# Expert weights laid out by the host in six 1 MB pieces, each loaded by one transfer with 8 KB in a row for each partition

## The chip, the cores and the metric

The kernel runs on one core of a Trainium2 chip. The metric is the device time of one execution in microseconds (us). Names of engines: PE multiplies matrices, DVE and ACT work element by element, POOL is the general-purpose engine (it also issues the indirect transfers), SP issues all other transfers. The data move on 16 DMA engines that the queues share.

## What is computed

One decoder layer on 2048 tokens of width 1024. A token mixer (gated linear attention and a gated delta rule, joined by an output projection) is followed by a layer norm; then comes a mixture of experts, and a second layer norm. The change touches the experts alone, whose reference, cut, is:

```python
D_MODEL, N_EXPERTS, TOP_K, D_EXPERT = 1024, 64, 2, 512

def expert_block(blk):                  # up to 128 tokens that chose expert e
    xb, e = blk
    hid = jax.nn.silu(xb @ w_gate[e]) * (xb @ w_up[e])
    return hid @ w_down[e]
...
y = jnp.einsum('nkd,nk->nd', y_assign, gate)      # two experts a token
x = _layer_norm(ALPHA_DN * x + y, ln2_g[l], ln2_b[l])
```

Everything is float32. One expert has 2 MB in each of `w_gate` (1024 x 512), `w_up` (1024 x 512) and `w_down` (512 x 1024), so that all 64 experts have 384 MB, and every one of them is read once.

## The kernel before

`mixer_front` and `mixer_out` compute the mixer, the first layer norm and the router, token tile by token tile. The last part of `mixer_out` (`project` and `route`, lines 860 to 925) loads for each tile of 128 tokens `ma`, `mb` (line 878) and `x` (line 880), multiplies by `w_out` (line 898), normalises, stores the row `x_d` (line 905) and transposes it for the router; POOL adds the bias of the norm (line 215) and scatters the tile's two routing entries a token into a table (`tab_d`, line 191).

**Experts.** `experts` runs through 52 tiles of up to 128 tokens: 3 for experts 0 to 2, then by falling size 6 tiles of three experts with two tiles each (a double), 28 of one expert (solo) and 15 tiles in which two experts with at most 64 tokens share the two halves of the partitions (a pair). A tile's stages: POOL gathers the tokens' rows (`xg<-x_d`, line 1344), PE transposes them and multiplies by gate and up (`gu`, line 1349), ACT and DVE form the hidden values, PE multiplies by down (`y`), DVE adds with the gate (line 1436), and POOL scatters the result (`y_d<-xg`, line 1439). Five buffers `xg` serve for gathering and for the result, so a gather waits for the scatter of five tiles before.

**Weights.** The class `Weights` cuts an expert into six pieces of [128, 4, 512] float32 (1 MB, 8 KB a partition). Pieces 0 to 3 hold two rows of gate and two of up for each partition, pieces 4 and 5 two rows of down. The order of loads (`load`, lines 1189 and 1193) and splits into a high and a low part (`split`, ACT at line 1203, then DVE or, for piece 5, POOL at line 1205) is written down beforehand by `slot_plan`: 20 slots of 1 MB are shared by pieces that are landing and by high and low parts, and a load waits until the last user of its slot is done. Pieces of a pair are used as they land, without a split. The first nine pieces are loaded inside `mixer_out`.

A piece of gate and up is loaded by two transfers, a piece of down by one:

```python
for j, w in enumerate((w_gate, w_up)):
    self.nc.sync.dma_start(raw[:, 2 * j:2 * j + 2, :],
                           w[e].rearrange("a (p k) c -> p (a k) c", k=8)
                           [:, 2 * i:2 * i + 2, :])
```

For gate and up, partition p owns eight rows of 2 KB in a row in DRAM (16 KB), of which a piece takes two, that is 4 KB. For down, partition p owns four rows of 4 KB, of which a piece takes two, 8 KB.

All of these transfers stand in SP's one queue, in the program's order. The program gives SP's transfers eight semaphores in turn, and a transfer is issued only after the one eight places before it has landed; so at most eight are under way. A scheduler orders each engine's instructions within the limits of the dependencies that the code lays down; the order of PE in the experts is fixed by hand.

At the end `overflow` treats blocks that did not fit the plan, in a loop whose count is read from memory, and `Final.norm` reads `y_d` (line 1575, 16 transfers of 1 MB with 8 KB in a row for each partition), adds and normalises.

Of the kernel before, what the change touches and what calls it, by code (L numbers as in the profile page):

```python
# [21 lines left out]
D = 1024  # L22
# [5 lines left out]
NE = 64  # L28
# [13 lines left out]
@with_exitstack  # L42
def hybrid_kernel(ctx, tc, x, w_in, w_gk_up, b_gk, conv_w, a_log, dt_bias, gla_norm_g, gdn_norm_g,
                  w_out, ln1_g, ln1_b, w_router_group, b_router_group, w_router_expert,
                  b_router_expert, w_gate, w_up, w_down, ln2_g, ln2_b, out, dbg=None, upto=9):
    nc = tc.nc
    dbg = dbg or {}
    dram = lambda name, shape, dt=F32: tc.dram_tile(shape, dt, name=name)
    dr = {n: dram(n + "_d", shape) for n, shape in (
        ("aT", [NT, 128, 4, 128]), ("bT", [NT, 128, 12, 128]), ("va", [NT, 128, 512]),  # L50
        ("ra", [NT, 128, 512]), ("zb", [NT, 128, 512]), ("ma", [NT, 128, 512]),
        ("mb", [NT, 128, 512]),
        ("na", [NT, 4, 128, 128]), ("at", [NT, 128, 512]), ("kd", [NT, 128, 512]),
        ("vp", [NT, 128, 512]), ("td", [2, NT, 4, 4, 32, 32]))}
    x1_d = dram("x1_d", [S, D])
    y_d = dram("y_d", [2 * S, D])
    tab_d = dram("tab_d", [S * NE, 2], I32)

    consts = ctx.enter_context(tc.tile_pool(name="consts", bufs=1))
    mixer = ctx.enter_context(ExitStack())  # L60
    mc = mixer.enter_context(tc.tile_pool(name="mixerc", bufs=1))
    jp = mc.tile([128, 128], I32, name="jp")
    nc.gpsimd.iota(jp, pattern=[[1, 128]], base=0, channel_multiplier=-1)
    ident = consts.tile([128, 128], F32, name="ident")
    nc.vector.tensor_scalar(ident, jp, 0.0, None, op0=OP.is_equal)
    gt = Gates(tc, nc, mc, jp, a_log, dt_bias)

    rt = Routing(tc, nc, consts, jp, tab_d)
    scan = Scan(nc, gt, mc, ident, dr)
    mixer_front(tc, nc, gt, scan, ident, x[0], w_in[0], conv_w[0], gla_norm_g, gdn_norm_g,  # L70
                w_gk_up[0], b_gk, dr)
    for n, t in dr.items():
        if n in dbg:
            nc.sync.dma_start(dbg[n], t)
    if upto <= 2:
        return
    late = ctx.enter_context(tc.tile_pool(name="late", bufs=1, side="right", reuse_waits="tile"))
    rt.row = late.tile([1, NE], I32, name="row")
    rt.more = late.tile([1, 257], I32, name="more")
    rt.list = late.tile([128, 1], I32, name="list0")  # L80
    land = ctx.enter_context(ExitStack())
    weights = Weights(tc, nc, land, w_gate[0], w_up[0], w_down[0])
    mixer_out(tc, nc, rt, scan, weights, ident, x[0], w_out[0], ln1_g, ln1_b, w_router_group[0],
              b_router_group, w_router_expert[0], b_router_expert, dr, x1_d)
    if "x1" in dbg:
        nc.sync.dma_start(dbg["x1"], x1_d)
    if "gates" in dbg:
        nc.sync.dma_start(dbg["gates"], rt.choice[:, :, :, 1].bitcast(F32))
    if upto <= 3:
        return  # L90
    mixer.close()
    weights.open("p5b", range(EARLY, EARLY + 9))
    blocks = land.enter_context(tc.tile_pool(name="blocks", bufs=1, reuse_waits="tile"))
    listing = Order(tc, nc, rt, ident, blocks)
    listing.rank()
    experts(tc, nc, rt, listing, weights, ident, x1_d, y_d, tab_d)
    land.close()
    fix = ctx.enter_context(tc.tile_pool(name="p7fix", bufs=1, side="right", reuse_waits="tile"))
    final = Final(nc, fix, ln2_g, ln2_b)
    overflow(tc, nc, rt.more, ident, w_gate[0], w_up[0], w_down[0], x1_d, y_d, tab_d)  # L100
    final.norm(tc, ident, y_d, out[0])


# [3 lines left out]
class Routing:  # L107
    def __init__(self, tc, nc, consts, jp, tab_d):
        f = lambda name, shape, dt=F32: consts.tile(shape, dt, name=name)
        self.tab = tab_d  # L110
        self.count = f("count", [128, 128])
        self.iota = self.count[:, :NE]
        self.choice = f("choice", [128, NT, 2, 2], I32)
        self.gates = self.choice[:, :, :, 1].bitcast(F32)
        nc.gpsimd.iota(self.choice[:, :, :, 0], pattern=[[256, NT], [1, 2]], base=0, channel_multiplier=2)
        self.known = f("known", [128, NT, 2])
        self.mine, self.base = f("mine", [128, NT, 2], BF16), f("base0", [128, NT])
        self.before = f("before", [128, 128], BF16)
        nc.vector.tensor_scalar(self.before, jp, 0.0, None, op0=OP.is_gt)
        self.ones = f("ones_b", [128, 128], BF16)  # L120
        nc.vector.memset(self.ones, 1.0)
        self.carry = [f(f"carry{i}", [128, NE]) for i in range(2)]
        nc.vector.memset(self.carry[0], 0.0)
        self.turn = 0
        self.slots = {}
        with tc.tile_pool(name="padp", bufs=1) as pool:
            ii = pool.tile([128, 128], I32, name="iota_i")
            nc.gpsimd.iota(ii, pattern=[[1, 128]], base=0, channel_multiplier=0)
            nc.vector.tensor_copy(self.count, ii)
            ki = pool.tile([128, NT, 2], I32, name="known_i")  # L130
            nc.gpsimd.iota(ki[:, :, 0], pattern=[[0, NT]], base=0, channel_multiplier=1)
            nc.gpsimd.iota(ki[:, :, 1], pattern=[[128, NT]], base=-2 * S, channel_multiplier=0)
            nc.vector.tensor_copy(self.known, ki)
            pad = pool.tile([128, 2 * S * NE // 128], I32, name="pad")
            nc.gpsimd.memset(pad, PAD)
            nc.sync.dma_start(flat(tab_d, [[2 * S * NE // 128, 128], [1, 2 * S * NE // 128]]), pad)
# [1026 lines left out]
class Weights:  # L1163


    def __init__(self, tc, nc, ctx, w_gate, w_up, w_down):
        self.tc, self.nc, self.ctx = tc, nc, ctx
        self.w = w_gate, w_up, w_down
        self.raw, self.where = {}, {}
        units = [(1, 1)] * FIRST + [(1 + (q[0] < DOUBLE), len(q)) for q in place_order()]  # L1170
        self.todo, uses = sequence(units)
        self.whole = [units[pos][1] == 2 for _, pos, _, _ in self.todo]
        self.events = slot_plan(uses, self.whole)
# [8 lines left out]

    def load(self, m, slot, e):
        raw = self.raw[m] = self.tile(slot, F32)
        w_gate, w_up, w_down = self.w
        e, i = ds(e, 1), self.todo[m][3]
        if i < 4:
            for j, w in enumerate((w_gate, w_up)):
                self.nc.sync.dma_start(raw[:, 2 * j:2 * j + 2, :],
                                       w[e].rearrange("a (p k) c -> p (a k) c", k=8)  # L1190
                                       [:, 2 * i:2 * i + 2, :])
        else:
            self.last = self.nc.sync.dma_start(
                raw.rearrange("p (k a) b -> p k (a b)", k=2),
                w_down[e].rearrange("a (p k) c -> p (a k) c", k=4)[:, 2 * (i - 4):2 * (i - 4) + 2, :]).ins

    def take(self, m):
        return self.raw.pop(m)
# [281 lines left out]
                fetch(n + 2)  # L1480


def overflow(tc, nc, row, ident, w_gate, w_up, w_down, x1_d, y_d, tab_d):

    with ExitStack() as es:
        fix = es.enter_context(tc.tile_pool(name="p6fix", bufs=1, reuse_waits="tile"))
# [3 lines left out]
        v = nc.vector  # L1490
# [3 lines left out]
        n = nc.values_load(row[0:1, 256:], min_val=0, max_val=2 * S // 128)  # L1494
        with tc.For_i(0, n) as i:
            e = nc.values_load(row[0:1, ds(2 * i, 1)], min_val=0, max_val=NE - 1)
# [4 lines left out]
            wu = [wts.tile([128, 2, D // 2], F32, name=f"ou{j}") for j in range(4)]  # L1501
            wg = [wts.tile([128, 2, D // 2], F32, name=f"og{j}") for j in range(4)]
            wd = [wts.tile([128, 2, D], F32, name=f"od{j}") for j in range(2)]
            for j in range(4):
                for t, w in ((wg[j], w_gate), (wu[j], w_up)):
                    nc.sync.dma_start(t, w[ds(e, 1)].rearrange("a (p k) c -> p (a k) c", k=8)
                                      [:, 2 * j:2 * j + 2, :])
            for j in range(2):
                nc.sync.dma_start(wd[j], w_down[ds(e, 1)].rearrange("a (p k) c -> p (a k) c", k=4)
                                  [:, 2 * j:2 * j + 2, :])  # L1510
            tok = work.tile([128, 1], I32, name="otok")
            v.tensor_scalar(tok, ids, 1, None, op0=OP.arith_shift_right)
            odd, res = work.tile([128, 1], I32, name="oodd"), work.tile([128, 1], F32, name="ores")
# [43 lines left out]
class Final:  # L1557
# [10 lines left out]
    def norm(self, tc, ident, y_d, out):  # L1568
# [44 lines left out]

_INS = ['x', 'w_in', 'w_gk_up', 'b_gk', 'conv_w', 'a_log', 'dt_bias', 'gla_norm_g', 'gdn_norm_g',
        'w_out', 'ln1_g', 'ln1_b', 'w_router_group', 'b_router_group', 'w_router_expert',
        'b_router_expert', 'w_gate', 'w_up', 'w_down', 'ln2_g', 'ln2_b']
_OUTS = [((1, 2048, 1024), 'float32')]


# [19 lines left out]
```

## Time and profile before

| | us |
|---|---|
| three runs | 2590.53, 2597.74, 2597.86 (median 2597.74) |
| profiled execution | 2591.04 |
| its span in the trace | 2589.3 |

| engine | busy in the span | share |
|---|---|---|
| PE | 2401.2 | 93% |
| DVE | 1645.1 | 64% |
| ACT | 1134.7 | 44% |
| POOL | 956.0 | 37% |
| SP's DMA queue (q1), share of 16 engines | | 69.0% |

In the page's 40 slices (64.7 us each) the DMA engines are 30 to 60% busy until 1424 us and 90% or more from 1489 us on; the rate rises from 100 to 235 GB/s there to about 390 GB/s. The experts run from about 1390 to 2510 us. In the whole span 305,902 packets moved 679.38 MB; 592.10 MB were read from HBM.

How to read it: the profile is of one execution. The busy time of PE is modelled, since products follow each other in a pipeline. A row of waits names who waited, for whom, how long in all and how often; "SPq" is SP as an issuer of transfers. The time to landing is from the issue of a transfer until its last byte is reported.

### The profile page before, as it was taken

Reading aid. Unit: us, or ns where it says so; the run is one execution under the profiler, and the core shown is the slowest. Engines: PE = TensorE matmul, PEld = TensorE weight load, DVE = VectorE, ACT = ScalarE, POOL = GpSimd, SP = SyncE. Lnnn points to the kernel's source line nnn. Section 1 sums busy time; section 2 is a strip of 40 time slices with the busy share of each in tenths; the row PEclk is TensorE's granted clock in tenths of the full one; section 3 lists DMA queues with packets and bytes.
Section 4 is the critical chain, followed back from the end, with each engine's and each line's share of the span. In section 5 each row is a group of like instructions: output and inputs, shape, how many; then the busy total and the mean of one; then the engine's idle time right before and its main releaser. Section 6 shows DMA issues by size and latency. Waiting matters only on the chain. (4 is left out here: it accounts for less than half of the span.)

```text
span 2589.3 us, 45456 instructions
## 1 busy us (share of the span) xinstructions
PE 2401.2 (93%) x16069; PEld 1807.7 (70%) x16069; DVE 1645.1 (64%) x3771; ACT 1134.7 (44%) x2211; POOL 956.0 (37%) x1006
## 2 busy tenths in 40 slices
PE   7898989999999998899996999999999999999978
PEld 6797769887978787788885766565557655566633
DVE  6746883787577866778898945445445554455517
ACT  3435443544554454522214745445444444455512
POOL 5222582234723561373223422233223322323316
PEclk9999999999989998899996999999999999999989
DMA  5465346645654556554364899999999999999978
GB/s 163 122 196 177 115 120 193 187 143 162 212 169 134 167 174 198 182 165 149 100 235 172 301 408 409 404 378 393 386 392 386 395 395 397 382 392 401 399 297 347
DMA packets 305902, 679.38 MB, mean 262 GB/s; under 512 B 48711, under 2 KB 168073, under 8 KB 287113
## 3 DMA queue, kind: packets, MB, share of 16 engines
q1 hardware_dynamic: 289832, 639.71, 69.0%
q0 software_dynamic: 15840, 36.76, 4.0%
q8 instruction: 127, 2.08, 0.3%
q14 instruction: 103, 0.84, 0.1%
HBM read 592.10 MB, written 98.27 MB: 267 GB/s over the span
## 5 line engine op out<-in xcount | busy, mean ns | idle before, releaser
L1349 PE MATMUL gu<-w,xh 128*128 128x512 f32 (+1 forms) x2144 | 552.5, 491 | 10.2 <-DMA w<-in_w_up_dram 5.4
L1205 DVE TENSOR_TENSOR w<-w,w 128x2048 fp32r<-128x2048 f32 x170 | 402.2, 2387 | 220.9 <-ACT w L1203 166.3
L1203 ACT ACTIVATE w<-w 128x2048 fp32r<-128x2048 f32 x204 | 389.3, 1916 | 309.4 <-PE gu L1349 125.1
L1349 PEld LDWEIGHTS gu<-w,xh 128*128 128x128 f32 (+1 forms) x2144 | 289.1, 167 | 205.0 <-issue 127.2
L1349 PE MATMUL y<-w,hh 128*128 128x512 f32 (+1 forms) x1072 | 283.7, 496 | 44.9 <-POOL w L1205 30.6
L1205 POOL TENSOR_TENSOR w<-w,w 128x2048 fp32r<-128x2048 f32 x34 | 158.0, 4647 | 419.3 <-ACT w L1203 355.9
L1349 PEld LDWEIGHTS y<-w,hh 128*128 128x128 f32 (+1 forms) x1072 | 143.8, 169 | 140.9 <-issue 58.2
L419 PE MATMUL mm<-xhi,whi 128*128 128x512 f32 x512 | 209.9, 410 | 20.0 <-ACT cr L431 19.9
L391 PE MATMUL mm<-whi,xhi 128*128 128x256 f32 (+2 forms) x768 | 226.6, 295 | 1.3 <-ACT oa L424 0.6
L372 POOL TENSOR_TENSOR wlo<-raw,whi 128x512 fp32r<-128x512 f32 (+2 forms) x112 | 151.0, 1349 | 204.3 <-ACT whi L371 202.0
L391 PE MATMUL mm<-whi,xlo 128*128 128x256 f32 (+2 forms) x768 | 220.6, 287 | 0.0
L391 PE MATMUL mm<-wlo,xhi 128*128 128x256 f32 (+2 forms) x768 | 220.3, 287 | 0.0
L419 PE MATMUL mm<-xlo,whi 128*128 128x512 f32 x512 | 207.9, 406 | 0.0
L371 ACT ACTIVATE whi<-raw 128x512 fp32r<-128x512 f32 (+2 forms) x224 | 132.5, 628 | 170.9 <-DMA raw<-in_w_in_dram 113.4
L419 PE MATMUL mm<-xhi,wlo 128*128 128x512 f32 x512 | 205.4, 401 | 0.0
L1439 POOL DMA_INDIRECT y_d<-xg,ids x52 | 88.8, 1707 | 281.9 <-DVE xg L1436 175.7
L1349 PE MATMUL gu<-w,xl 128*128 128x512 f32 x592 | 186.8, 397 | 4.4 <-DVE xl L1369 4.4
L372 DVE TENSOR_TENSOR wlo<-raw,whi 128x512 fp32r<-128x512 f32 (+2 forms) x112 | 102.8, 924 | 99.5 <-ACT whi L371 98.0
L391 PEld LDWEIGHTS mm<-whi,xhi 128*128 128x128 f32 x768 | 146.6, 191 | 6.5 <-issue 1.4
L391 PEld LDWEIGHTS mm<-whi,xlo 128*128 128x128 f32 x768 | 146.6, 191 | 2.4 <-issue 1.2
L391 PEld LDWEIGHTS mm<-wlo,xhi 128*128 128x128 f32 x768 | 146.6, 191 | 1.0 <-issue 0.2
L1436 DVE SCALAR_TENSOR_TENSOR xg<-y,gate,xg 128x512 f32<-128x512 f32 x104 | 74.7, 745 | 108.0 <-PE y L1349 107.7
(455 smaller groups left out, 4768.3 us busy)
## 6 DMA issues: line engine op xcount, KB each, us to landing
w<-in_w_gate_dram SPq DMA_DIRECT2D x256, 512.0 KB, 13.1
w<-in_w_up_dram SPq DMA_DIRECT2D x256, 512.0 KB, 11.5
w<-in_w_down_dram SPq DMA_DIRECT2D x128, 1024.0 KB, 13.8
raw<-in_w_in_dram SPq DMA_DIRECT2D x192, 256.0 KB, 3.1
y<-y_d SPq DMA_DIRECT2D x16, 1024.0 KB, 17.9
bT_d<-oa SPq DMA_DIRECT2D x48, 256.0 KB, 2.5
bT<-bT_d SPq DMA_DIRECT2D x16, 768.0 KB, 5.7
xt<-in_x_dram SPq DMA_DIRECT2D x32, 256.0 KB, 4.5
```

What stands on the lines that cost most here:

```text
L371: nc.scalar.activation(hi[:, ks, :n], raw, AF.Copy)
L372: (nc.gpsimd if h % 2 else nc.vector).tensor_sub(lo[:, ks, :n], raw, hi[:, ks, :n].bitcast(F32))
L391: nc.tensor.matmul(p[:, :n], xs[:, k, j * 128:(j + 1) * 128], ws[:, k, :n], start=(m == 0), stop=(m == 3 * KD - 1))
L419: nc.tensor.matmul(p, ws[:, k, s * 128:(s + 1) * 128], xs[:, k, :nt], start=(m == 0), stop=(m == 3 * KD - 1))
L1203: cp = self.nc.scalar.activation(full(hi), full(raw), AF.Copy)
L1205: sub = engine.tensor_sub(full(lo), full(raw), full(hi).bitcast(F32))
L1349: mm = lambda *args, **kw: tc.keep_in_program_order(nc.tensor.matmul(*args, **kw))
L1436: nc.vector.scalar_tensor_tensor(yt[:, cs], py[j], col.gate[:, c:c + 1], yt[:, cs], op0=OP.mult, op1=OP.add)
L1439: nc.gpsimd.indirect_dma_start(out=y_d, out_offset=bass.IndirectOffsetOnAxis(ap=col.ids[r, c:c + 1], axis=0), in_=yt[r], in_offset=None, b ...
```

## The change

The host stacks the three tensors into one, `w_experts` of [64, 6, 128, 2048]: piece i of expert e is 1 MB in a row, 8 KB for each partition in the order in which the tile holds it. `load` issues one transfer for any piece. `overflow` reads the same tensor with views of a piece's halves. What lands in each slot, and everything computed from it, is unchanged, and so are the tables of loads, splits and slots.

```diff
 class Weights:
-    def __init__(self, tc, nc, ctx, w_gate, w_up, w_down):
-        self.tc, self.nc, self.ctx = tc, nc, ctx
-        self.w = w_gate, w_up, w_down
+    def __init__(self, tc, nc, ctx, w_experts):
+        self.tc, self.nc, self.ctx, self.w = tc, nc, ctx, w_experts
...
     def load(self, m, slot, e):
         raw = self.raw[m] = self.tile(slot, F32)
-        w_gate, w_up, w_down = self.w
-        e, i = ds(e, 1), self.todo[m][3]
-        if i < 4:
-            for j, w in enumerate((w_gate, w_up)):
-                self.nc.sync.dma_start(raw[:, 2 * j:2 * j + 2, :],
-                                       w[e].rearrange("a (p k) c -> p (a k) c", k=8)
-                                       [:, 2 * i:2 * i + 2, :])
-        else:
-            self.last = self.nc.sync.dma_start(
-                raw.rearrange("p (k a) b -> p k (a b)", k=2),
-                w_down[e].rearrange("a (p k) c -> p (a k) c", k=4)[:, 2 * (i - 4):2 * (i - 4) + 2, :]).ins
+        self.last = self.nc.sync.dma_start(raw.rearrange("p a b -> p (a b)"), self.w[ds(e, 1), self.todo[m][3]]
+                                           .rearrange("a p c -> p (a c)")).ins
...
+def laid_out(inputs, np):
+
+    a = {n: np.ascontiguousarray(v) for n, v in inputs.items()}
+    gu = np.stack([a.pop(n).reshape(NE, 128, 4, 2 * 512) for n in ('w_gate', 'w_up')], 3)
+    d = a.pop('w_down').reshape(NE, 128, 2, 2 * D)
+    a['w_experts'] = np.concatenate([gu.reshape(NE, 128, 4, 2 * D).transpose(0, 2, 1, 3),
+                                     d.transpose(0, 2, 1, 3)], 1)
+    return a
```

The scheduler makes another order of the changed program in the last tiles of `mixer_out`; in the experts the order of PE, ACT, DVE and POOL stays but for a few neighbours that change places. Three places follow.

SP in the experts, pieces 3, 4 and 5 of one expert (an ISA row sets up the address of the transfer behind it). Before:

```order
L1189 DMA w_18440<-in_w_gate_dram 128x1024
L1189 ISA
L1189 DMA w_18440<-in_w_up_dram 128x1024
L1193 ISA
L1193 DMA w_18443<-in_w_down_dram 128x2048
```

And in the change, three pieces in a row:

```order
L1184 DMA w_18399<-in_w_experts_dram 128x2048
L1184 ISA
L1184 DMA w_18401<-in_w_experts_dram 128x2048
L1184 ISA
L1184 DMA w_18403<-in_w_experts_dram 128x2048
```

A piece of gate and up takes one transfer of the form that a piece of down had; SP has six transfers an expert where it had ten.

SP in the last tiles of `mixer_out`, behind the first five pieces. Before:

```order
L1189 DMA w_16667<-in_w_up_dram 128x1024
L878 DMA ma<-ma_d 128x512
L878 DMA mb<-mb_d 128x512
L880 DMA x<-in_x_dram 128x1024
L1189 DMA w_16848<-in_w_gate_dram 128x1024
L1189 DMA w_16848<-in_w_up_dram 128x1024
L905 DMA x_d<-x_16462 128x1024
```

In the change:

```order
L1184 DMA w_16663<-in_w_experts_dram 128x2048
L878 DMA ma<-ma_d 128x512
L880 DMA x<-in_x_dram 128x1024
L1184 DMA w_16843<-in_w_experts_dram 128x2048
L878 DMA mb<-mb_d 128x512
L905 DMA x_d<-x_16459 128x1024
```

The load of `mb` has moved behind that of `x` and of one more piece.

POOL in the same tiles (`x<-u,ln1b` is the bias of the norm, `tab_d<-choice` the scatter of routing entries). Before:

```order
L215 TENSOR_TENSOR x_16281<-u,ln1b 128x1024
L191 DMA tab_d<-choice,sl 131072x2 x2
L215 TENSOR_TENSOR x_16462<-u,ln1b 128x1024
L191 DMA tab_d<-choice,sl 131072x2
L215 TENSOR_TENSOR x_16643<-u,ln1b 128x1024
L191 DMA tab_d<-choice,sl 131072x2 x3
L215 TENSOR_TENSOR x_16824<-u,ln1b 128x1024
```

In the change:

```order
L215 TENSOR_TENSOR x_16279<-u,ln1b 128x1024
L191 DMA tab_d<-choice,sl 131072x2
L215 TENSOR_TENSOR x_16459<-u,ln1b 128x1024
L191 DMA tab_d<-choice,sl 131072x2
L215 TENSOR_TENSOR x_16639<-u,ln1b 128x1024
L191 DMA tab_d<-choice,sl 131072x2 x4
L215 TENSOR_TENSOR x_16819<-u,ln1b 128x1024
```

Two additions stand one scatter earlier, and four scatters stand together where there were three.

## Rows read from the trace of the kernel before

**Rows 1.** By stage: stretch, us, busy PE, PEld, DVE, ACT, POOL, clock, DMA, GB/s

```profile
1300.00:1350.00 50.00, 49.69 (x272) 41.60 (x271) 45.24 (x163) 8.27 (x22) 16.98 (x11) 1.00 0.70 266
1480.00:2490.00 1010.00, 956.92 (x4348) 613.97 (x4348) 506.33 (x404) 472.65 (x397) 286.16 (x122) 0.99 1.01 394
```

**Rows 2.** Chain that ended last, 1480 to 2490 us (start, us, what)

```profile
1949.30 2.58 PE y L1349 x10
...
2038.91 15.20 DMA w<-in_w_down_dram
...
2226.49 3.78 PE y L1349 x10
...
2297.97 0.90 PE xt L1350 x8
```

**Rows 3.** SP's queue, 1480 to 2490: who waited for whom, us, times, longest

```profile
SPq L1189 <- DMA w<-in_w_down_dram: 257.2, 113, 4.5
...
SPq L1193 <- POOL w L1205: 8.5, 2, 5.0
```

**Rows 4.** DMA view of 1480 to 2490 (packets below a size include the smaller ones)

```profile
DMA packets 95627, 398.26 MB, mean 394 GB/s; under 512 B 13558, under 2 KB 13559, under 8 KB 80545
q1 hardware_dynamic: 83817, 366.71, 92.7%
q0 software_dynamic: 11744, 30.73, 8.2%
```

**Rows 5.** DMA view of 1548:1558, 1614:1626, 1838:1848, 1909:1921, 2119:2129, 2186:2201

```profile
DMA packets 1110, 4.10 MB, mean 410 GB/s; under 512 B 122, under 2 KB 122, under 8 KB 1100
...
DMA packets 1306, 4.79 MB, mean 399 GB/s; under 512 B 147, under 2 KB 147, under 8 KB 1295
...
DMA packets 1054, 3.89 MB, mean 389 GB/s; under 512 B 116, under 2 KB 116, under 8 KB 1045
...
DMA packets 1246, 4.59 MB, mean 383 GB/s; under 512 B 135, under 2 KB 135, under 8 KB 1236
...
DMA packets 1064, 3.90 MB, mean 390 GB/s; under 512 B 121, under 2 KB 121, under 8 KB 1056
...
DMA packets 1664, 6.11 MB, mean 407 GB/s; under 512 B 186, under 2 KB 186, under 8 KB 1651
```

**Rows 6.** DMA view of 1513:1521, 1951:1961 and 2228:2238

```profile
DMA packets 471, 3.35 MB, mean 418 GB/s; under 512 B 54, under 2 KB 54, under 8 KB 71
...
DMA packets 578, 4.18 MB, mean 418 GB/s; under 512 B 64, under 2 KB 64, under 8 KB 71
...
DMA packets 573, 4.13 MB, mean 413 GB/s; under 512 B 64, under 2 KB 64, under 8 KB 73
```

**Rows 7.** DMA view of 2525:2555, in the final norm

```profile
DMA packets 1736, 12.65 MB, mean 422 GB/s; under 512 B 192, under 2 KB 192, under 8 KB 192
```

**Rows 8.** DMA issues of the whole span: count, KB each, us to landing

```profile
w<-in_w_gate_dram SPq DMA_DIRECT2D x256, 512.0 KB, 13.1
w<-in_w_up_dram SPq DMA_DIRECT2D x256, 512.0 KB, 11.5
```

**Rows 9.** Splits in 1480 to 2490: busy us, mean ns, idle before and its releasers

```profile
L1205 DVE TENSOR_TENSOR w<-w,w 128x2048 fp32r<-128x2048 f32 x148 | 343.7, 2344 | 201.1 <-ACT w L1203 146.5 <-DMA w<-in_w_up_dram 34.7 <-POOL w L1205 10.4
L1203 ACT ACTIVATE w<-w 128x2048 fp32r<-128x2048 f32 x177 | 337.8, 1916 | 287.9 <-PE gu L1349 115.5 <-DMA w<-in_w_down_dram 80.6 <-DMA w<-in_w_up_dram 33.7
L1205 POOL TENSOR_TENSOR w<-w,w 128x2048 fp32r<-128x2048 f32 x30 | 139.6, 4652 | 382.3 <-ACT w L1203 319.0 <-DMA w<-in_w_gate_dram 35.1 <-PE gu L1349 25.3
```

**Rows 10.** Waits of PE and POOL, 1480 to 2490

```profile
PE y L1349 <- POOL w L1205: 30.6, 15, 3.0
...
POOL xg L1344 <- DMA y_d<-xg,ids: 48.9, 10, 8.3
```

**Rows 11.** POOL in the last tiles of the mixer (start, us, ..., idle before)

```profile
1328.64 1.68 POOL L191 DMA_INDIRECT tab_d<-choice,sl  x1 [4.36 <-DMA tab_d<-choice,sl]
1330.35 2.39 POOL L215 TENSOR_TENSOR x<-u,ln1b 128x1024 f32<-128x1024 f32 x1
```

More of the change, by code (lines that the diff above doesn't have):

```diff
@@ L44, in hybrid_kernel @@
                   w_out, ln1_g, ln1_b, w_router_group, b_router_group, w_router_expert,
-                  b_router_expert, w_gate, w_up, w_down, ln2_g, ln2_b, out, dbg=None, upto=9):
+                  b_router_expert, w_experts, ln2_g, ln2_b, out, dbg=None, upto=9):
     nc = tc.nc
@@ L81, in hybrid_kernel @@
     land = ctx.enter_context(ExitStack())
-    weights = Weights(tc, nc, land, w_gate[0], w_up[0], w_down[0])
+    weights = Weights(tc, nc, land, w_experts)
     mixer_out(tc, nc, rt, scan, weights, ident, x[0], w_out[0], ln1_g, ln1_b, w_router_group[0],
@@ L99, in hybrid_kernel @@
     final = Final(nc, fix, ln2_g, ln2_b)
-    overflow(tc, nc, rt.more, ident, w_gate[0], w_up[0], w_down[0], x1_d, y_d, tab_d)
+    overflow(tc, nc, rt.more, ident, w_experts, x1_d, y_d, tab_d)
     final.norm(tc, ident, y_d, out[0])
@@ L1480, in experts, with overflow @@
                 fetch(n + 2)
-def overflow(tc, nc, row, ident, w_gate, w_up, w_down, x1_d, y_d, tab_d):
+def overflow(tc, nc, row, ident, w_experts, x1_d, y_d, tab_d):
     with ExitStack() as es:
@@ L1503, in overflow @@
             wd = [wts.tile([128, 2, D], F32, name=f"od{j}") for j in range(2)]
+            piece = lambda i: w_experts[ds(e, 1), i].rearrange("a p (h k c) -> p (a h) k c", h=2, k=2)
             for j in range(4):
-                for t, w in ((wg[j], w_gate), (wu[j], w_up)):
-                    nc.sync.dma_start(t, w[ds(e, 1)].rearrange("a (p k) c -> p (a k) c", k=8)
-                                      [:, 2 * j:2 * j + 2, :])
+                nc.sync.dma_start(wg[j], piece(j)[:, 0])
+                nc.sync.dma_start(wu[j], piece(j)[:, 1])
             for j in range(2):
-                nc.sync.dma_start(wd[j], w_down[ds(e, 1)].rearrange("a (p k) c -> p (a k) c", k=4)
-                                  [:, 2 * j:2 * j + 2, :])
+                nc.sync.dma_start(wd[j], w_experts[ds(e, 1), 4 + j].rearrange("a p (k c) -> p (a k) c", k=2))
             tok = work.tile([128, 1], I32, name="otok")
@@ L1615 @@
         'w_out', 'ln1_g', 'ln1_b', 'w_router_group', 'b_router_group', 'w_router_expert',
-        'b_router_expert', 'w_gate', 'w_up', 'w_down', 'ln2_g', 'ln2_b']
+        'b_router_expert', 'w_experts', 'ln2_g', 'ln2_b']
 _OUTS = [((1, 2048, 1024), 'float32')]
+def laid_out(inputs, np):
[5 more added lines that the diff above has]
+    return a
 def kernel(**inputs):
@@ L1626 @@
     arrays, args = {}, []
+    inputs = laid_out(inputs, _np)
     for name in _INS:
-        a = _np.ascontiguousarray(inputs[name])
+        a = inputs[name]
         arrays[f"in_{name}_dram"] = a
```

## The prediction

> **What bounds the kernel now.** I read the busy time by stage first. From 1480 to 2490 us, 1010 of the 2589.3 us of the span, the DMA engines are busy all the time (share 1.01) at 394 GB/s, while PE has 956.92 us of work, DVE 506, ACT 473 and POOL 286 [rows 1]. So in this stretch there are two candidates, the DMA engines without a gap and PE with 53 us of gaps (1010 - 956.92). Before 1480 us the DMA engines are not full, and there a faster transfer has little to give.
>
> The chain of waits is the second view. In the stretch it consists mostly of transfers of `w`, but not only: from 1949.30 to 2038.91 us it runs on PE through five tiles without waiting for a weight, and then goes over to the landing of a piece of down; from 2226.49 to 2298.87 us it does so again [rows 2]. These two stretches, 162 us together, lie around a double, whose second tile uses the weights of the first. PE lags there, and the transfers run ahead of it. The third view tells whether they ever have to stop: SP waits almost only for a transfer of its own queue to land (257.2 us in the largest row); the largest wait for a slot, which POOL's split frees, sums up to 8.5 us [rows 3]. The queue is thus always full, and the 1010 us are as long as the bytes take. That makes the price of a byte the quantity to find.
>
> **The price of 4 KB and of 8 KB in a row.** In the stretch 95,627 packets moved, of which 80,545 are under 8 KB; the other 15,082 are of 8 KB and carry 123.6 MB, the pieces of down. SP's queue moved 366.71 MB, so 243.1 MB of it went in packets of 4 KB, the pieces of gate and up [rows 4]. I looked for stretches of at least 8 us in which one kind is nearly alone and POOL's queue is silent. Six stretches of 4 KB packets have 383 to 410 GB/s, together 27.38 MB in 69 us, 396.8 GB/s [rows 5]. Three of 8 KB packets have 413 to 418 GB/s, together 11.66 MB in 28 us, 416.4 GB/s [rows 6]. The completion packets (under 512 B), of which 4 KB packets need twice as many for their bytes, are inside these rates. In the final norm, with 1 MB in a row a transfer as in the new layout, the rate is 422 GB/s [rows 7].
>
> **The change, part by part.**
> - *Gate and up in one transfer with 8 KB in a row.* 512 transfers of 512 KB become 256 of 1 MB [rows 8]. The 243.1 MB take 612.7 us at 396.8 GB/s and 583.8 us at 416.4 GB/s: 28.9 us less. The six rates scatter by about 10 GB/s, hence their mean by about 4, and the three by 2 in the mean; that is 7 us either way, so 22 to 36 us. The widest ends are set by single stretches: 410 against 413 GB/s gives 4 us, 383 against 418 gives 53 us. I take 29 us, since the sums rest on 69 and 28 us.
> - *Down, read from 1 MB in a row instead of 8 KB out of every 16 KB.* Its packets stay as they are: 0. Its nearest rows are the 416.4 GB/s of now and the 422 GB/s of the final norm, where nothing else runs; 123.6 MB would gain 4 us. I keep 0 to 4 us.
> - *SP's issues.* Four of ten transfers an expert go, with their address setting. SP waits for landings anyway [rows 3], so this is hidden: 0. With eight transfers of 1 MB under way instead of a mix, up to 8 MB stand in the queue, and the time to landing rises from 11 to 13 us [rows 8] to about 20 us (8 times 1.05 MB at 416 GB/s). A piece does not land later for it, since the bytes ahead of it are the same; it is issued sooner, until slots and no longer landings hold SP back. What is late next is a free slot, hence the split: 1.92 us on ACT, then 2.34 us on DVE or 4.65 us on POOL a piece [rows 9], against 2.5 us for the transfer of a piece. Each of these engines has half of the stretch free [rows 1].
> - *Whether PE can follow.* The gain needs gaps of PE to shrink from 53 to about 24 us. Around the doubles the transfers must run ahead as they do now; SP's waits leave room for it [rows 3]. If the lead cannot be stored there, the gain counts only outside the 162 us in which the chain stands on PE: 29 x 848 / 1010 = 24 us, which lies inside the 22 to 36 us.
> - *The new order in the last tiles of the mixer.* `mb` lands a little later, PE has other products ahead of it, and in 1300 to 1350 us it is busy 49.69 of 50 us [rows 1], so they cover it: 0; without that cover it would cost about one piece, 2.5 us. On POOL two additions stand one scatter earlier and then one scatter more stands ahead of another; such a scatter waits 4.36 us for the one before it, the addition takes 2.39 us [rows 11]. I take 0, with ends of -4 and +4 us.
> - *Overflow, gathers, scatters, final norm.* Nothing changes in their instructions: 0.
>
> The sum is -29 us, from -15 to -44 us with all bounds, against the profiled execution's 2591.04 us (span 2589.3): 2562 us. That execution lies with the lowest of the three runs (2590.53), 6.7 us below the median of 2597.74. Two of the four known times are at either level, so I add half of the distance: **2565 us**.
>
> [...]
>
> **The rivals.**
> 1. *A larger gain.* All of SP's queue runs at the rate of the final norm: 398.26 MB at 422 GB/s would take 944 us, 66 us less, but PE's work of 956.92 us then ends the stretch at 53 us less at best: 2538 us on the profiled scale. For it: reading from 1 MB in a row, and fewer long stalls. Against it: POOL's 30.73 MB stay in 4 KB packets, and three stretches of 8 KB packets in the present layout have almost that rate already, so that little of it can come from the layout. Chance 0.12.
> 2. *The rate depends on bytes, not on packets.* The slower 4 KB stretches are slow because of what the engines do at that time (383 and 389 beside 410 GB/s), and 8 KB packets put there are as slow. As a mechanism of this kernel: from the best 4 KB rate, 410, to 416.4 GB/s the 243.1 MB gain 9 us at most, about half of it if the two kinds differ as the closest single stretches do (410 and 413): 2582 to 2587 us on the profiled scale. A part of this rival is that the change does not do what it says, and the new transfers are cut into 4 KB after all, time 2591 us; against it, down has the same form, 128x2048, and goes in 8 KB. Together 0.11. [...]
> 3. *Slower: POOL's gathers and scatters pass more slowly beside 8 KB packets.* A tile of 128 rows has eight 4 KB packets on each DMA engine. If each must let one of SP's packets pass, it waits 8 x 0.31 instead of 8 x 0.165 us (8 KB and 4 KB at 26 and 25 GB/s an engine, from the rates above), 1.2 us more. POOL waits for scatters before it gathers (48.9 us), POOL's split of piece 5 stands behind that in the same queue, and PE waits for that split 15 times, 30.6 us [rows 10]. If every one of the 47 tiles in the stretch lost 1.2 us on this path, that is 56 us, 27 us more than the gain: 2618 us. It decides only if POOL's wait reaches PE in more than half of the tiles, where it now does in 15 of 47 with 2 us each, and POOL is idle for 70% of the stretch. Chance 0.05.
>
> **How the numbers follow.** The forecast has 0.72, with its own range of 2551 to 2580 us. A measurement of this kernel can tell about 0.3% from no change, 8 us. Faster by more are the forecast and rival 1: 0.84. Within 8 us is rival 2, whose times lie 9 to 0 us under the profiled one: 0.11. Slower is rival 3: 0.05. The range reaches from rival 1 to just short of no change, 2538 to 2589 us, and leaves out rival 3, the wider half of rival 2 and the tails.
>
> **What would show it.** Right: the packets of the span fall by 32,768 and by 4,096 completions, to about 269,000; the stretch from about 1480 us ends some 29 us earlier with the DMA share still at 1.0 and 404 to 408 GB/s instead of 394; one group of 384 transfers of 1 MB lands in 15 to 21 us; SP's waits move in part from landings to splits and PE; PE's gaps fall to about 24 us. Wrong in size: the DMA share falls under 0.98 (PE or the splits hold the slots), or the rate of stretches with weights alone stays under 405 GB/s. Wrong in sign: POOL's waits for scatters grow well beyond 100 us and PE's wait for POOL's split with them.

## The result, and the profile after

The changed kernel takes 2573.11 us (median of 6 runs, 2561.93 to 2576.90), the kernel before in the same comparison 2595.45 (6 runs, 2585.76 to 2600.81). The ratio is 0.9916, 95% interval 0.9891 to 0.9941, which is 15 to 28 us less. The profiled execution of the change took 2570.79 us (span 2569.1) against 2591.04 (span 2589.3).

The page of the change, DMA part and issues (count, KB each, us to landing), which answers to [rows 8]:

```profile
DMA packets 269031, 679.31 MB, mean 264 GB/s; under 512 B 44615, under 2 KB 163977, under 8 KB 217481
...
q1 hardware_dynamic: 252968, 639.69, 68.0%
...
w<-in_w_experts_dram SPq DMA_DIRECT2D x384, 1024.0 KB, 21.2
```

The bytes are those of before and the packets fell from 305,902 to 269,031, as counted in advance: gate and up now go in packets of 8 KB. A piece takes 21.2 us from issue to landing.

By stage the profile of before, cut at 2470 us because the experts of the changed kernel end soon after:

```profile
1480.00:2470.00 990.00, 938.13 (x4268) 607.98 (x4270) 505.58 (x403) 472.40 (x396) 286.16 (x122) 0.99 1.01 394
```

and the profile of the change, with the stretch in the mixer too, for [rows 1]:

```profile
1300.00:1350.00 50.00, 47.55 (x261) 39.02 (x260) 39.56 (x154) 8.29 (x21) 15.58 (x11) 1.00 0.64 249
1480.00:2470.00 990.00, 951.62 (x4349) 620.50 (x4349) 510.73 (x407) 476.38 (x399) 289.08 (x123) 0.98 1.00 403
```

In the same 990 us PE is busy 13.5 us longer and the DMA engines move 403 instead of 394 GB/s. The difference lies in the experts. Their bounds are two instructions of SP, the store of the list of slots ahead of them and the first load of `y` behind them. The timeline of before (start, us):

```profile
1392.20 0.53 SPq L1033 DMA_DIRECT2D list_d<-wi  x1
...
2516.48 23.81 SPq L1575 DMA_DIRECT2D y<-y_d  x16
```

and that of the change:

```profile
1395.92 0.52 SPq L1033 DMA_DIRECT2D list_d<-wi  x1
...
2495.70 23.85 SPq L1564 DMA_DIRECT2D y<-y_d  x16
```

By stage between these bounds, before:

```profile
1392.20:2516.48 1124.28, 1050.75 (x4747) 686.32 (x4747) 588.79 (x511) 535.56 (x447) 330.79 (x143) 0.98 0.97 377
```

and in the change, with the same 4747 products:

```profile
1395.92:2495.70 1099.78, 1041.87 (x4747) 687.97 (x4747) 588.99 (x511) 535.82 (x447) 331.92 (x143) 0.97 0.96 385
```

The experts take 1099.78 instead of 1124.28 us, 24.5 less: PE's gaps shrink by 15.6 us (from 73.5 to 57.9), and its busy time by 8.9. They begin 3.7 us later, and what follows them takes 0.6 us more (73.4 against 72.8 to the end of the span); together 20.2 us, the difference of the spans.

What SP waits for in the change, 1480 to 2490 us:

```profile
SPq L1184 <- DMA w<-in_w_experts_dram: 571.2, 271, 4.4
SPq L1184 <- DVE w L1195: 129.0, 50, 7.8
SPq L1184 <- POOL w L1195: 47.9, 11, 9.3
```

The waits for landings of a weight shrank only from the 634 us of five rows before to 571, but those for a split, at most 8.5 us in any row before [rows 3] and 20.9 us in all four such rows, are now 177 us. Waits of PE and POOL in the same stretch, which answer to [rows 10]:

```profile
PE y L1339 <- POOL w L1195: 33.3, 15, 2.7
...
POOL xg L1334 <- DMA y_d<-xg,ids: 53.3, 10, 8.6
```

They have grown by 2.7 and 4.4 us, with the same counts. The wait for POOL's split is most of what PE still lacks: its gaps in 1480 to 2470 us are 38.4 us (990 - 951.62), and the landing of a weight is no longer among the waits that the trace names for them (5.9 us before).

### The profile page after: what moved, and what is told of

It is laid out like the page before. It is cut to its first block, busy times and chain, and to the rows that moved or that the text cites. A ratio compares the mean times of both kernels' runs of the same rounds, so it can differ in the third digit from the quotient of the medians.

```text
span 2569.1 us, 44565 instructions
## 1 busy us (share of the span) xinstructions
PE 2399.1 (93%) x16069; PEld 1813.1 (71%) x16069; DVE 1641.4 (64%) x3771; ACT 1135.3 (44%) x2211; POOL 956.3 (37%) x1006
## 2 busy tenths in 40 slices
DMA packets 269031, 679.31 MB, mean 264 GB/s; under 512 B 44615, under 2 KB 163977, under 8 KB 217481
## 5 line engine op out<-in xcount | busy, mean ns | idle before, releaser
L1339 PE MATMUL gu<-w,xh 128*128 128x512 f32 (+1 forms) x2144 | 545.5, 489 | 0.0
L1195 DVE TENSOR_TENSOR w<-w,w 128x2048 fp32r<-128x2048 f32 x170 | 401.9, 2383 | 184.9 <-ACT w L1193 168.0
L1339 PE MATMUL y<-w,hh 128*128 128x512 f32 (+1 forms) x1072 | 283.0, 497 | 38.2 <-POOL w L1195 33.3
## 6 DMA issues: line engine op xcount, KB each, us to landing
w<-in_w_experts_dram SPq DMA_DIRECT2D x384, 1024.0 KB, 21.2
```

The lines of the kernel that those rows point to most:

```text
L1195: sub = engine.tensor_sub(full(lo), full(raw), full(hi).bitcast(F32))
L1339: mm = lambda *args, **kw: tc.keep_in_program_order(nc.tensor.matmul(*args, **kw))
```

## The experiments

Three things change at once: a gate and up packet grows from 4 to 8 KB (the theory), a piece lies in one place in DRAM (rival: the layout), and it comes in one transfer instead of two (rival: the number of transfers). The first runs hold two of the three fixed. Diffs are against the change; each ratio is to the kernel before on the same chip.

**Layout alone.** Two transfers of half a partition's row each, so 4 KB packets again; the order on PE, DVE, ACT and POOL is that of the kernel before.

```diff
-        self.last = self.nc.sync.dma_start(raw.rearrange("p a b -> p (a b)"), ...
+        full, piece = raw.rearrange("p a b -> p (a b)"), ...
+        for c in (slice(0, D), slice(D, 2 * D)) if self.todo[m][3] < 4 else (slice(0, 2 * D),):
+            self.last = self.nc.sync.dma_start(full[:, c], piece[:, c]).ins
```

> Each piece of gate and up lies in 1 MB in a row as in the change, but is fetched by two transfers of 512 KB with 4 KB a partition; pieces of down as in the change. The order of PE, DVE, ACT and POOL is word for word that of the kernel before. Theory P (the price is a packet's: 169 ns for 4 KB, 322 ns for 8 KB): nothing won, ratio to the kernel before 0.997 to 1.003, rate in the full stretch 392 to 397 GB/s. Rival L (the gain comes from reading 1 MB in a row): ratio 0.990 to 0.994, 403 GB/s. Rival N (the gain comes from fewer transfers): ratio 1.000, as P.

Measured: 2586.29 us, ratio 0.9982 [0.9967, 0.9998]. The DMA view of 1500 to 2460 us of this kernel:

```profile
DMA packets 91085, 379.07 MB, mean 395 GB/s; under 512 B 12992, under 2 KB 12992, under 8 KB 76711
```

against that of the kernel before:

```profile
DMA packets 90864, 378.51 MB, mean 394 GB/s; under 512 B 12905, under 2 KB 12905, under 8 KB 76491
```

and of the change:

```profile
DMA packets 60461, 387.31 MB, mean 403 GB/s; under 512 B 9546, under 2 KB 9546, under 8 KB 16892
```

The layout moves the rate by 1 GB/s where the change moves it by 9. By the interval's middle it is worth 0.2%, by its end 0.3%; the interval only just leaves out no change at all.

**One transfer, packets of 4 KB.** The host stores a piece as its gate half and then its up half, each with 4 KB for a partition; one transfer takes both. PE, DVE, ACT and POOL have the order of the change.

```diff
+            self.last = self.nc.sync.dma_start(raw.rearrange("p (h k) b -> p h (k b)", h=2),
+                                               piece.rearrange("a (h p c) -> p (a h) c", h=2, p=128)).ins
```

> One transfer a piece as in the change, but a piece lies in DRAM as the gate half of all partitions and then the up half, so that the packets have 4 KB. The order of the four engines is word for word that of the changed kernel. Theory P: the price of before and the changed kernel's later start of the experts (3.7 us): ratio to the kernel before 0.998 to 1.004, 392 to 397 GB/s. Rival N (fewer transfers): ratio 0.990 to 0.994, as the change. Rival L: 0.990 to 0.994.

Measured: 2593.62 us, ratio 1.0003 [0.9987, 1.0019]; 1500 to 2460 us:

```profile
DMA packets 88378, 381.21 MB, mean 397 GB/s; under 512 B 9557, under 2 KB 9558, under 8 KB 74204
```

The whole time is that of theory P. The profiled execution is the longest of the twelve (2604.28 us), and its list of slots is stored late, at 1412.80 us; what the experts take in it is read further down.

**One transfer, packets of 2 KB.** The same with four parts.

```diff
+            self.last = self.nc.sync.dma_start(raw, piece.rearrange("a (h p c) -> p (a h) c", h=4, p=128)).ins
```

> As the run before, but a piece of gate and up lies in DRAM in four parts, so that its packets have 2 KB. Theory P, with a fixed part of 15.5 ns a packet from 169 and 322 ns: 2 KB cost 92 ns, 8 KB in four packets 369 instead of 338 ns in two, 32768 x 31 ns / 16 engines = 63 us more than the kernel before, 2640 to 2660 us, ratio 1.018 to 1.026. With 86 ns, which packets of 2 KB took in the mixer's last part of the kernel before, 13 us more, ratio 1.005. Rival N: ratio 0.990 to 0.994.

Measured: 2621.27 us, ratio 1.0110 [1.0086, 1.0133]:

```profile
DMA packets 140854, 370.51 MB, mean 386 GB/s; under 512 B 9165, under 2 KB 9165, under 8 KB 126893
```

The ratio lies between the two values expected (1.005, and 1.018 to 1.026): theory P has the sign and not the size, and rival N falls. These two and the change have one order, one number of transfers and 1 MB in a row for a piece; only the packet differs. With 2, 4 and 8 KB the rates are 386, 397 and 403 GB/s, the times 2621, 2594 and 2573 us and the ratios 1.0110, 1.0003 and 0.9916.

The mean duration of a packet of SP's queue, over the packet records of 1500 to 2460 us, is 90.4 ns for 2 KB (this trace), 168.9 for 4 KB (that of before) and 322.6 for 8 KB (that of the change): two packets of 4 KB take 15.2 ns more than one of 8 KB, and two of 2 KB 11.9 ns more than one of 4 KB. 243.1 MB are 59,350 packets of 4 KB, hence 29,675 savings of 15.2 ns on 16 engines: 28 us, near the price of the prediction (29).

Between runs that differ in the packet alone the saving is smaller: 13.4 ns with one transfer a piece (168.0 ns in the run before this one, against 322.6) and 12.0 ns with two (168.2 ns in the first run, against 324.4 in the run with even and odd partitions below), 22 to 25 us. This is time of the engines and not yet time of the kernel: the records of packets overlap (their share is 1.03 of the time with 2 KB), and an engine that is done sooner can stand idle (the gaps of the DMA engines, read further down, sum to 9.1 us before and 13.6 in the change). By the whole time fewer transfers, with 1.0003, give nothing that can be told.

**Two transfers with packets of 8 KB.** If packets are the cause, two transfers should keep the gain. First by halves of the partitions.

```diff
+        for p in (slice(0, 64), slice(64, 128)) if self.todo[m][3] < 4 else (slice(0, 128),):
+            self.last = self.nc.sync.dma_start(full[p], piece[p]).ins
```

> The change's layout and its 8 KB packets, but a piece of gate and up is fetched by two transfers of 64 partitions each, so that there are as many transfers as before; the order of the engines is nearly that of the kernel before (16 of 12513 instructions of PE differ). Theory P: the gain of the change and a start of the experts that is not 3.7 us later: ratio 0.988 to 0.993, 403 GB/s. Rival N: ratio 0.998 to 1.002, 394 GB/s.

Measured: 3343.72 us, ratio 1.2893 [1.2859, 1.2927], which neither theory had. The DMA view of 1500 to 2460 us:

```profile
DMA packets 36911, 219.64 MB, mean 229 GB/s; under 512 B 7800, under 2 KB 7801, under 8 KB 12445
```

The engines are busy (share 0.98 in 1480 to 2470 us), but an 8 KB packet takes 560 ns in the mean, against 322.6 in the change. Whether this comes from 64 partitions that lie side by side or from 64 partitions as such, no view shows. The next run puts it to the test: same bytes, packets and number of transfers, but even and then odd partitions.

```diff
+        for p in (slice(0, 128, 2), slice(1, 128, 2)) if self.todo[m][3] < 4 else (slice(0, 128),):
```

> As the run with two transfers of 64 partitions, but the first takes the even partitions and the second the odd ones. If the 29% of that run came from its 64 partitions lying side by side (half of the memory's width written at a time), a packet of 8 KB takes 322 ns again; then theory P says ratio 0.988 to 0.993 with as many transfers as before, and rival N (the number of transfers) 0.998 to 1.002. If a transfer over 64 partitions is slow in itself, ratio above 1.2 again.

Measured: 2574.06 us, ratio 0.9935 [0.9906, 0.9965]:

```profile
DMA packets 63765, 385.79 MB, mean 402 GB/s; under 512 B 13087, under 2 KB 13087, under 8 KB 20335
```

So the choice of partitions was the whole loss: with even and odd partitions, two transfers a piece reach 402 GB/s, and an 8 KB packet takes 324 ns. Why a packet takes longer with neighbouring partitions was not shown. Beside the first run, with the same number of transfers and the same layout but 4 KB, the rate rises by 7 GB/s and the ratio falls from 0.9982 to 0.9935. The packet is a cause from this side too.

**What each part is worth, by stage.** The whole time contains the start of the experts, which scatters (see below). Their length, from the store of the list to the first load of `y`, separates the parts better. Layout alone (1121.3 us):

```profile
1399.34 0.52 SPq L1033 DMA_DIRECT2D list_d<-wi  x1
...
2520.68 23.61 SPq L1565 DMA_DIRECT2D y<-y_d  x16
```

One transfer, packets of 4 KB (1115.4 us):

```profile
1412.80 0.52 SPq L1033 DMA_DIRECT2D list_d<-wi  x1
...
2528.22 23.99 SPq L1571 DMA_DIRECT2D y<-y_d  x16
```

Two transfers of even and odd partitions, packets of 8 KB (1103.5 us):

```profile
1385.57 0.48 SPq L1033 DMA_DIRECT2D list_d<-wi  x1
...
2489.03 23.10 SPq L1565 DMA_DIRECT2D y<-y_d  x16
```

Between 1124.3 us before and 1099.8 us in the change, the layout thus has 2.9 us, one transfer instead of two 5.9 us (with 4 KB) or 3.7 us (with 8 KB), and the packet 17.9 us (with two transfers) or 15.6 us (with one). The bytes moved in 1500 to 2460 us, in the DMA views above, divide alike: of the 8.8 MB that the change moves more than the kernel before, 0.6 come with the layout, 2.1 or 1.5 with the single transfer and 6.7 or 6.1 with the packet. The packet is the main cause, with two thirds to three quarters of the gain, and not the only one. Each length is of one profile (the change has two, of equal length), so the 2.9 us of the layout are the least certain.

**The order in the mixer.** In the change's profile the experts begin 3.7 us later. Here the pieces loaded in the mixer come in two transfers, which gives PE, DVE, ACT and POOL the order of the kernel before; all later pieces are as in the change.

```diff
+        two = m < EARLY + 5 and self.todo[m][3] < 4
+        for c in (slice(0, D), slice(D, 2 * D)) if two else (slice(0, 2 * D),):
```

> The change, but the pieces of gate and up among the first 14 are fetched by two transfers with 4 KB a partition, as before; this gives back the order of PE, DVE, ACT and POOL of the kernel before, word for word. Theory O (the scheduler's other order in the last tiles of the mixer starts the experts 3.7 us later): the expert list is stored at about 1392 instead of 1396 us, ratio to the kernel before 0.988 to 0.991, 3 to 5 us under the change. Rival (the later start is chance of that execution, or is made up later): list at 1395 to 1397 us or ratio 0.991 to 0.993.

Measured: 2571.15 us, ratio 0.9913 [0.9880, 0.9946]. The list is stored at 1398.24 us, later still than in the change, and not at 1392 as theory O had it; so the 3.7 us of one profile are no proof that the order costs them. The experts take 1098.3 us, as in the change (1099.8).

**The missing 5 us around the doubles.** In steps of 5 us from 1500 to 2460 us I summed what the DMA share lacks to 1.015, the share of a full stretch: 9.1 us before, 13.6 in the change. The two stretches below lie in those that the prediction named. By stage, before:

```profile
1975.00:1990.00 15.00, 15.00 (x71) 12.40 (x70) 10.58 (x7) 11.37 (x10) 7.46 (x2) 1.00 0.98 364
...
2250.00:2290.00 40.00, 40.00 (x189) 33.06 (x188) 30.61 (x24) 27.64 (x22) 10.48 (x5) 1.00 1.00 375
```

and in the change:

```profile
1975.00:1990.00 15.00, 15.00 (x72) 12.46 (x72) 14.47 (x10) 8.70 (x9) 5.89 (x3) 1.00 0.87 325
...
2250.00:2290.00 40.00, 40.00 (x186) 32.97 (x185) 28.83 (x23) 23.62 (x22) 13.25 (x6) 1.00 0.90 332
```

PE is busy all the time in both, but the DMA share falls to 0.87 and 0.90. SP's waits in 2245 to 2295 us of the change:

```profile
SPq L1184 <- DVE w L1195: 25.1, 7, 7.8
SPq L1184 <- POOL w L1195: 8.2, 2, 4.9
SPq L1184 <- DMA w<-in_w_experts_dram: 4.3, 2, 3.1
```

The next transfer waits for a split that frees a landed piece's slot; before, SP waited 0.4 us for a split in the same stretch. The kernel with one transfer and 4 KB packets lacks 9.5 us, and the one with two transfers and 8 KB packets, at 402 GB/s, 10.7 us: neither makes the gap of the change alone. A second profile of the change (below) lacks 15.0 us. Two kernels split pieces four and three uses ahead instead of five (`READY`), so that a piece stays longer in the slot in which it landed.

```diff
-        for m in uses[now + 1:now + 1 + (READY if loads < total else total)]:
+        for m in uses[now + 1:now + 1 + (4 if loads < total else total)]:
```

> The change, with pieces split for the next four uses instead of five, so that one slot more holds a piece that lands. Theory S (around the doubles the lead of the transfers finds no slot, some 8 us): the DMA engines' gaps at about 1680, 1980 and 2250 us shrink by 2 to 3 us each, ratio to the kernel before 0.987 to 0.990. Rival (the split then comes too late for PE): PE's waits for ACT, DVE and POOL grow by more than 10 us in the stretch, ratio 0.992 or more.

Measured: 2571.91 us, ratio 0.9920 [0.9888, 0.9951]; the gaps sum to 18.1 us. Theory S falls, since they grow; the rival's cause does not show either, since PE's waits for splits, 36.7 us in the change, are 35.1.

> The change, with splits three uses ahead: two slots more for landing pieces. Theory S: gaps of the DMA engines around the doubles gone but for 2 us, ratio 0.986 to 0.990. Rival: PE waits for splits, 20 us and more, ratio 0.995 or above.

Measured (with 3 in that line): 2579.53 us, ratio 0.9946 [0.9921, 0.9971]; gaps 29.9 us. SP's waits in 1480 to 2490 us:

```profile
SPq L1184 <- DMA w<-in_w_experts_dram: 363.8, 176, 4.3
SPq L1184 <- DVE w L1195: 300.5, 82, 20.8
```

Later splits lengthen the waits for DVE's split (129.0, then 300.5 us) and the gaps. Four ahead costs nothing in time, three ahead some 8 us against it. PE's waits for splits stay at 36.4 us, so three ahead is not slower by the rival's cause. The other side, six ahead:

> The change with pieces split six uses ahead instead of five; the same transfers and the same work. Theory G (what is missing around the doubles is a slot that is freed in time): a piece leaves its landing slot one use sooner, the gaps of DMA shrink below 13.6 us, SP's waits for splits fall below 120 us in the stretch from 1480 to 2490 us, ratio 0.988 to 0.991. Rival R (a slot used for a split piece is one less for a landing piece, the total is what counts): gaps the same or larger, ratio 0.991 to 0.995.

Measured: 2577.59 us, ratio 0.9942 [0.9924, 0.9960], gaps 15.8 us (13.6 and 15.0 in the two profiles of the change), waits for splits 146.2 (DVE) and 49.1 us (POOL). No gain: the part of this theory that an earlier split frees the slot soon enough falls; the rival said so, since the split piece needs a slot too.

**The place of the doubles.** The 20 slots stay, and each double moves by one place, to stand directly ahead of a pair.

```diff
+            if q < DOUBLE and n + 1 >= (q + 1) * (rest // (DOUBLE + 1)):
+                order.append((q,))
+                q += 1
...
-        if (n + 1) % (rest // (DOUBLE + 1)) == 0 and q < DOUBLE:
-            order.append((q,))
-            q += 1
```

> The change with the three doubles moved by at most two places in the order of the work, so that each stands directly before a pair; the same transfers and the same work. Theory G (part of the gain is lost around the doubles, because the transfers' lead there fills all slots): a lead made of a pair's pieces or used up sooner leaves fewer gaps, those of DMA shrink from about 13.6 us to under 9 us, and the ratio to the kernel before falls from 0.9916 to 0.989 to 0.991. Rival R (the lead is limited in any order): gaps of 12 us or more, ratio 0.991 to 0.994.

Measured: 2582.98 us, ratio 0.9960 [0.9943, 0.9978]; the gaps grew to 25.9 us. Theory G had the wrong sign; rival R had 12 us or more right, but the time lies above its range. By stage, around the three doubles of this kernel:

```profile
1705.00:1735.00 30.00, 30.00 (x136) 24.66 (x135) 14.98 (x13) 12.31 (x12) 17.00 (x7) 0.95 0.79 309
...
1935.00:1965.00 30.00, 26.18 (x113) 21.10 (x112) 10.91 (x10) 8.95 (x8) 17.78 (x7) 0.94 0.73 272
...
2210.00:2225.00 15.00, 15.00 (x72) 12.44 (x71) 10.59 (x9) 7.10 (x8) 10.33 (x4) 1.00 0.71 273
```

The run shows that the place of a double decides how much is lost there: 11 to 12 us more gaps at the same packets, slots and work, and 7 us more time than the change in the same comparison (2576.02, below), nearly all of it in the experts (1106.6 against 1099.8 us). SP's waits for POOL's splits grow from 47.9 to 107.5 us, those for DVE's hardly (129.0 to 137.2). Why a pair behind the double is worse is argued, not shown: here two solos stand ahead of each double, where the change has one solo ahead of the first of them and a pair directly ahead of the other two. A solo needs 15 us of transfers (six pieces of 2.5 us) and a pair 30, against 956.92 / 47 = 20 us of PE a tile, so solos lengthen the lead with which the double begins, and a pair shortens it.

**The change once more.**

> The change itself once more, for the chance in a single profile. Theory O2 (a profile's start of the experts scatters by several us from execution to execution, their length by 1 to 2 us): the list of slots is stored somewhere between 1385 and 1400 us, and from there to the first gather after the experts it is 1098 to 1102 us (1099.8 in the first profile of the change), ratio 0.989 to 0.994. Rival: the list is stored at 1395 to 1397 us again, 3 to 5 us later than in the kernel before, as a lasting cost of the new order in the mixer.

Measured, in the same comparison as the last two: 2576.02 us, ratio 0.9938 [0.9914, 0.9962]. The list is stored at 1401.23 us and `y` first loaded at 2501.03: 1099.8 us again. The length of the experts repeats to 0.1 us. Their beginning does not repeat, and was later than either side had said.

## Why the prediction was right, and where a term was off

- **Sign, mechanism and total: right.** 2565 was forecast, 2573 measured, within the range. What bounded the experts was the time of a packet on the DMA engines, and the packet of 8 KB brings most of the gain (15.6 to 17.9 of the 24.5 us by which the experts got shorter). Layout alone, and layout with a single transfer, leave the whole time within 0.2% of before.
- **The price, -29 us: right as time of the engines, too large as time of the kernel.** The two rates, read from stretches of the old trace [rows 5, 6], gave 29 us; the durations of packets give 22 to 28. Where the packet alone differs, the experts differ by 15.6 to 17.9 us. The forecast of 404 to 408 GB/s over the stretch was missed by a little (403), and only 6 to 7 of the 9 GB/s gained are the packet's.
- **SP's issues, 0: too small.** Fewer transfers were put at nothing because SP waits for landings anyway. By stage one transfer instead of two shortens the experts by 3.7 to 5.9 us. The cause stays open; the completion packets of the stretch fall with the transfers (12,992 to 9,557). The layout, 0 to 4 us, has 2.9.
- **"SP's waits leave room for it": the step that failed.** Small waits for slots [rows 3] showed that the slots were enough at the old rate, and not that some were left over. At the new rate SP reaches their end around each double, and over the stretch the DMA engines lose 4.5 us more than before (13.6 - 9.1; 5.9 by the second profile). The prediction had the case, as "if the lead cannot be stored there, the gain counts only outside": 24 us. That this agrees with the 24.5 us by which the experts got shorter is in part luck, since about 7 to 9 us of these come from the single transfer and the layout, and the packet gave less than the 24.
- **The order in the mixer, 0 with ends of -4 and +4: left open.** In the two profiles of the change the experts begin 3.7 and 9.0 us later than in that of before. Where PE, DVE, ACT and POOL have the order of before, or nearly, other profiles have 1385.6, 1398.2 and 1399.3 us (and 1417.1 in the run at 229 GB/s); where they have that of the change, 1395.9 to 1412.8 in eight. A cost of some 4 us, the difference between the 24.5 us and the 20 us of the spans, fits these, and so does the run with one transfer and 4 KB, whose experts are 8.9 us shorter and whose whole time is that of before; but the run with the old order and the new transfers (0.9913) cannot be told from the change (0.9916, 0.9938).
- **PE's gaps: right in kind, too large in size.** They were to shrink by 29 us and shrink by 15.6 over the experts. Another 8.9 us come from PE's busy time, which the prediction held fixed; why the same products are busy for less was not tried. The granted clock does not explain it: it is not higher in the change (0.97) than before (0.98).
- **Landing, 15 to 21 us:** 21.2, just past the end of the range. Up to eight transfers of 1 MB are now under way: in 21.2 us at 403 GB/s 8.5 MB move.
- **Rival 1 (larger gain)** falls: layout alone moves the rate by 1 GB/s. **Rival 2 (bytes, not packets)** falls by the three packet sizes in one order: 2 KB cost 28 us over 4 KB, and 8 KB win 17 to 23 by the ratios (1.0003 against 0.9938 and 0.9916). **Rival 3 (POOL beside larger packets)** falls: POOL's wait for its scatters went from 48.9 to 53.3 us and PE's for POOL's split from 30.6 to 33.3.
- No kernel of the study is measurably faster than the change; the best ratios (0.9913, 0.9916, 0.9920) are the same within their intervals.

## What to carry to other kernels

Read the price of a packet from stretches in which one size runs alone, and multiply the difference by the bytes: here that gave about the engines' time (29 us against 22 to 28), of which 15.6 to 17.9 us became time of the kernel. When a change touches packet size, layout and number of transfers at once, vary them one by one, and compare the length of the stage: the whole time hid what the single transfer gave. Then look where the faster stream will run into the end of its buffers; a wait for a free slot that is small because the stream is slow is not room (SP's waits for splits: 20.9 us before, 177 in the change). When a transfer is split, look at the partitions of each part too: here two transfers of even and of odd partitions moved 402 GB/s, two of neighbouring halves 229.

## What the runs showed that was not expected

- Two transfers of 64 neighbouring partitions, 8 KB each, move 229 GB/s where even and odd partitions move 402, with 560 against 324 ns for a packet; up to eight such transfers under way at a time (22.9 us in the median from issue to landing) did not make up for it.
- The beginning of the experts moves between 1385 and 1413 us over the profiles, with nothing changed ahead of it but the order of a few instructions and the form of the first pieces' loads (1417 with the run at 229 GB/s), while the length of the experts of one kernel repeats (1099.8 us twice).
